# Half of a depthwise convolution by scaled copies and adding transfers, in a two-layer decoder trunk

## The chip, the cores and the metric

The kernel runs on one core of a Trainium2 chip. The metric is the time of one execution on the device in microseconds (us). The kernel before took 1113.77 us in the median of 3 runs (1112.04 to 1114.65).

The core has five engines with queues of their own, which work side by side and wait for each other by semaphores: TensorE (PE in the profile) multiplies matrices, VectorE (DVE) and ScalarE (ACT) work elementwise, GpSimd (POOL) does so more slowly, and SyncE (SP) issues transfers. ScalarE and GpSimd can issue transfers too. Each queue is worked off in its order: an instruction that waits holds up all behind it on its engine.

## The reference

The program is a decoder trunk of two layers over 528 tokens (512 and 16 learned ones in front) with 1024 channels. The first layer's mixer runs forgetting attention (8 heads of 64) beside a convolution branch; the second's pools over windows. Behind each stands a gated MLP. The part that matters here is the convolution branch, with 512 channels and 31 taps:

```
a, g = jnp.split(glu, 2, axis=-1)
u = a * jax.nn.sigmoid(g)
u = causal_depthwise_conv(u, conv_w, conv_b)     # 31 taps, each channel by itself
u = jax.nn.silu(layer_norm(u, ln_g, ln_b))       # mean and variance over the 512 channels
return jnp.concatenate([attn, u], axis=-1) @ w_out.astype(h.dtype)
```

All of it is in float32, and the sum over the taps of a channel is

```
out[c, t] = b[c] + sum over j of w[j, c] * u[c, t - 30 + j],   j = 0 .. 30
```

## The kernel before

Channels lie on the 128 partitions, tokens along the free dimension. The 512 channels of the convolution are four groups of 128, numbered 0 to 3; `u[i]` is a group's gated input with 30 zeros in front, `cv[i]` its sum. `cv[0]` to `cv[3]` are the tiles of the residual `h[0]` to `h[3]`, which are free meanwhile; in the rows below they are called `h_64` to `h_67`, so `h_65` is group 1 and `h_67` group 3, and `u_235` and `u_237` are their inputs.

All products of float32 matrices are made of three products of high and low parts. Each block of eight 128x128 weight tiles comes by one transfer of 512 KB (`raw`), is cut to its high part `wH` on ScalarE or VectorE, and its low part `wL` is the difference, on VectorE or, for the blocks listed in `POOL_CHUNKS`, on GpSimd (line 178). Most blocks of the first layer are in that list. Blocks are prepared two ahead of their use.

TensorE's order in the first layer is written out by hand. First come eight tiles of the gated input (`a` and `g` of the groups in turn, 16 half tiles), then by `PE_ORDER` 24 half tiles of queries, keys and values (F), between them the steps of the attention, and the steps of the layer norm of the convolution: SUM, MEAN, VAR, SILU. MEAN is a matmul with ones over the sum of the four `cv` tiles; it stands behind the last F. The output projection (O) follows. The instructions of the other engines are ordered by a scheduler.

When a group's gated input is ready (`done_g`, line 478), its 31 taps are entered in one of two lists. List 0 is VectorE's: one instruction for a tap, `cv = u * w + cv` (line 494). List 1 is for ScalarE with GpSimd: a product on ScalarE into a buffer `tapp`, of which there are two (line 497), and an addition to `cv` on GpSimd (line 498). The first tap of a group is on ScalarE in either case, with the bias (line 492). Groups 0 and 2 are in list 0, group 1 in list 1, and of group 3 the first 3 taps (`TAPS3`) are in list 1 and the other 28 in list 0. That makes 88 taps on VectorE and 32 additions on GpSimd.

The taps are drawn from the lists by `fill`, behind each half tile of a projection: `PACE` says how many from each list, with one pair of numbers for the gated stage and one for each later part of `PE_ORDER`. SUM draws what is left, and the sums over the groups follow on GpSimd (lines 757 and 767).

Of the kernel before, what the change touches and what calls it, by code (L numbers as in the profile page):

```python
# [52 lines left out]
# output projection in two passes: (tile of the output, tiles of the contraction)  # L53
OUT_ORDER = [(m, (0, 1, 2)) for m in range(8)] + [(m, (4, 5, 6, 7, 3)) for m in range(8)]
# first tile of the output projection whose halves take PSUM from both pools
OUT_WIDE = 3
OUT_JOINT = 1
# tiles of the convolution branch split by VectorE alone
SPLIT_V = (0, 3)
POOL_CHUNKS = (6, 7, 8, 10, 13, 14, 15, 16, 17, 18, 19, 20, 21, 22, 23, 24, 25, 28, 31, 34, 97, 98, 100, 101, 102, 104, 105, 106, 107)  # L60
# what the tensor engine does after the gated tiles. F: half a tile of an input projection, O: of the
# output projection; steps of the attention by pair of heads; a stroke: the next entry of PACE.
# [4 lines left out]
# first tiles of an up projection that go through the contraction side by side; tiles that leave PSUM  # L67
# before the norm is known
OUTER = (0, 4)
RAW = (7, 7)  # L70
# last tiles of the output, done by halves of the tokens; their stores: first and last tile, whether GpSimd
# computes them, whether ScalarE's queue takes them
HALVED = (6, 7)
OUT_PARTS = (((0, 4, 1, 0), (4, 8, 0, 1)), ((0, 1, 0, 0), (1, 3, 0, 1), (6, 8, 1, 0), (3, 6, 0, 1)))
# loads at the start: the input tile behind which the gate's weights are split, behind which the first
# weights come, the weights in front of which the table comes, tiles split by VectorE alone
START = (0, 0, 2, (1, 5))
# tiles of the pooling whose residual sum goes to GpSimd
POOL_RES = (1, 2, 3, 4, 5, 7)
POOL_Z = (1, 4, 6)  # L80
# tiles that the norm scales by halves as it comes
# [3 lines left out]
# steps of the pooling by tile: scale by the norm, window, its first tokens, residual, the next product  # L85
POOL_ORDER = ("Z0 Z1 S0 T1 D0 S1 Z2 T0 Z3 X0 S3 S2 D1 T2 T3 D2 X1 D3 Q0 Z4 Z5 S4 S5 X2 T4 T5 D4 Z6 X3 D5 Z7 "
              "S6 X4 Q2 Q5 Q1 S7 T7 T6 X5 D6 D7 X6 Q4 Q3 Q6 X7 Q7")
# taps of the convolution begun behind half a tile of a projection, on VectorE and on ScalarE with GpSimd
PACE = ((0.75, 0.25), (3.75, 5.0), (2.5, 4.5), (5.25, 1.25), (4.0, 1.0), (3.25, 3.0))
# squares of the last tiles that go to the norm by themselves: before the mixer, the MLPs and the pooling  # L90
# [4 lines left out]
# engines of the copies for a pair of heads: q twice, k twice, v (A: ScalarE, V: VectorE, P: GpSimd)  # L95
COPIES = ('AAAAA', 'VAAAV', 'APAAA', 'PAPAV')
# weight chunks whose high part VectorE takes
VECTOR_CHUNKS = (2, 3, 6, 9, 10, 14, 26, 27, 29, 30, 31, 33, 34, 96, 100, 101, 102, 105, 106, 107)
# products of constants that raise the tensor engine's clock while the first loads run
WARM = 12  # L100
# taps of the last tile of channels that go to GpSimd
TAPS3 = 3


def weight_order():
    """Order in which the tensor engine takes the 128x128 weight tiles."""
# [21 lines left out]
def trunk_kernel(  # L128
# [70 lines left out]
    def product(ps, wants, act, t0, n, first=True, final=True):  # L199
        """ps[:, half, :n] = sum over the wanted weight tiles of weight.T @ act."""  # L200
# [25 lines left out]
    def after(late, early):  # L226
        """Issue late behind early on their engine."""
        tc.add_manual_dep(late.ins, early.ins.name,
                          mybir.DependencyInfo(mybir.DependencyClass.NoSync, mybir.DependencyReason.DATA),
                          reason="order")  # L230

    def use_log_exp(early):
        """The table set with both Ln and Exp, loaded behind the instruction early."""
        ld = nc.scalar.preload_act_table_set("natural_log_exp_and_others")
        after(ld, early)
        return ld

# [1 line left out]
    def squares(m, apart, t0=0, t1=T, part=True):  # L239
        """Adds the squares of h[m] to the running sum, split at its end; the last ones stay apart."""  # L240
# [15 lines left out]
    def scaled(m, gcol, t0=0):  # L256
        """xH + xL = h[m] * g, split exactly."""
# [10 lines left out]
    def rsqrt(out, srcs, scale, bias, follow=None):  # L268
        """out = (scale * src + bias) ** -0.5: exp(-ln/2) and a Newton step. srcs: pieces in PSUM;
        follow(out, columns) comes behind each."""  # L270
# [24 lines left out]
    def inv_rms(pss, t0, early=(), follow=None):  # L295
        """R[:, token] = 1/sqrt(mean square + eps) in every partition."""
# [5 lines left out]
    # ================= layer 0: attention and convolution =================  # L302
    with ExitStack() as mx:
# [12 lines left out]
        # the gate's weights: high parts in columns 0:8, low parts from column 32 on  # L316
        # (in the memory of the attention's values, which come later)
# [24 lines left out]
        # causal masks, side by side as the blocks of the scores lie in PSUM (128 columns, 16 zeros, 128):  # L342
        # upper triangles for the maxima, lower ones for keys on partitions
# [5 lines left out]
        # the residual is read again after the mixer: until then its tiles serve as scratch  # L349
# [7 lines left out]
        # tokens on partitions: values of two heads with ones (high parts) or zeros (low) between  # L357
        # the last 16 tokens: high, high and low parts of the values below each other against high, low
        # and high parts of the weights
# [5 lines left out]
        # stacked operands of the scores. Even heads: rows 0:64 | 64:128  # L365
        #   q1 = high | low   k1 = high | high   q2 = high | decay rows   k2 = low | decay rows
        # odd heads have the two row halves exchanged.
# [53 lines left out]
        def mtile(name, wants, acts, done, alloc=(pp, pp), split_last=False):  # L421
            """Two units, one for each half of the tokens; done(half, psum) follows each."""
            ws = []
            def joint():
                """Both halves, the last weights behind the others of both."""
# [41 lines left out]
        def done_g(i):  # L467
            t_ = wk.tile([P, T], F32, tag="sq", name=f"sg{i}")

            def fn(hf, ps):  # L470
# [5 lines left out]
                if hf == 1:  # L476
                    uu = u[i][:, CW - 1:]
                    nc.gpsimd.tensor_tensor(uu, uu, t_, op=ALU.mult)
                    for j in range(CW):
                        queue[i % 2 if i < 3 or j < TAPS3 else 0].append((i, j))  # L480
# [8 lines left out]
        def tap(i, j, kind):  # L489
# [5 lines left out]
            else:  # L495
                pr = wk.tile([P, T], F32, tag="tapp", name=f"tap{i}_{j}")
                nc.scalar.activation(pr, src, AF.Copy, scale=cw(i, j))
                nc.gpsimd.tensor_tensor(cv[i], cv[i], pr, op=ALU.add)

        def fill(pace):  # L500
            for kind in range(2):
                credit[kind] = min(credit[kind] + pace[kind], len(queue[kind]))
                while credit[kind] >= 1:
                    tap(*queue[kind].pop(0), kind)
                    credit[kind] -= 1

# [1 line left out]
        def first_products():  # L508
            """The gates' logits and the first tile, as their operands come in."""
            cell["f"] = wk.tile([P, T], F32, tag="tapp", name="f")[H8, :]  # L510
            low = wk.tile([P, T], F32, tag="tapp", name="flow")[H8, :]
# [18 lines left out]
        def gate_sums():  # L530
# [6 lines left out]
            # log1p(e) = ln(1+e) + (e - ((1+e) - 1)) / (1+e)  # L537
# [62 lines left out]
        def attention(p):  # L600
            """The steps of a pair of heads by name."""
# [22 lines left out]
            # Maxima, queries on partitions. The query's own decay is the same for all its keys: it  # L624
            # stands in a row's scores and in their maximum alike, and their difference is free of it.
            def maxima(hh):
                tl = st[hh]
                N = tl["N"]
                for x, parts in enumerate((((2, 0, 272), (1, 0, 144), (0, 0, 16)), ((3, 0, 400),),
# [10 lines left out]
                    # short products in front of those whose weights load fast  # L640
# [3 lines left out]
                    # the masks cover the last columns of every block  # L644
# [32 lines left out]
            # Scores, keys on partitions; blocks of 128 keys against their causal queries.  # L677
# [517 lines left out]
```

## Time and profile before

| | |
|---|---|
| median of 3 runs | 1113.77 us (1112.04 to 1114.65) |
| span of the profiled execution, first to last instruction | 1111.1 us |
| TensorE busy | 1044.2 us, 94% |
| VectorE busy | 767.9 us, 69% |
| ScalarE busy | 467.4 us, 42% |
| GpSimd busy | 250.3 us, 23% |
| VectorE's taps, line 494 | 88, 1157 ns in the mean |
| GpSimd's additions of taps, line 498 | 32, 1566 ns in the mean |

The profiled execution is another one than the timed runs; its own time is known as its span, and the median of the runs lies 2.7 us above it. Busy shares are means over the span; the first layer's mixer, which has the convolution, takes the first 264 us or so.

How to read it: a row names the line of the program, the engine, the operation and the tiles, output in front of the arrow and inputs behind it. "x88" is a count. What stands in brackets or behind a second bar is the idle time of the engine before, and who ended it.

### The profile page before, as it was taken

How to read it: one execution, taken by the hardware profiler on the slowest of the kernel's cores; microseconds unless marked ns; L12 is line 12 of the kernel's file. 1: busy time of each engine (PE TensorE's matmuls, PEld its weight loads, DVE VectorE, ACT ScalarE, POOL GpSimd, SP SyncE). 2: the span in 40 equal slices, each digit the busy share in tenths (PEclk: the TensorE clock that was granted, in tenths of full speed). 3: DMA queues.
4: the chain of work that ended last, by engine and by line, in shares of the span. 5: the costliest groups of instructions: out<-in, count | busy, mean ns of one | idle time of the engine just before them, and what ended most of it. 6: DMA issues, size and time to landing. Idle time of an engine off the chain costs nothing. (4 is left out here: it accounts for less than half of the span.)

```text
span 1111.1 us, 19833 instructions
## 1 busy us (share of the span) xinstructions
PE 1044.2 (94%) x8356; PEld 1031.0 (93%) x8356; DVE 767.9 (69%) x1001; ACT 467.4 (42%) x710; POOL 250.3 (23%) x264
## 2 busy tenths in 40 slices
PE   8978699799999999999999999679999999999996
PEld 7877589799999999999999999579999999999995
DVE  7899999997727985236767546957985336767523
ACT  6435465465325553124434435333553124344422
POOL 7656766342500000000000013662000000000012
PEclk8988889999999999999999999899999999999998
DMA  6211111132332222332322222122322222222202
GB/s 222 68 56 57 39 39 40 58 98 75 104 108 96 87 87 94 96 95 79 95 95 89 84 96 77 38 77 77 112 88 91 91 96 95 96 96 81 92 20 76
DMA packets 28665, 93.21 MB, mean 84 GB/s; under 512 B 3616, under 2 KB 5664, under 8 KB 28576
## 3 DMA queue, kind: packets, MB, share of 16 engines
q1 hardware_dynamic: 26720, 90.68, 24.9%
q8 instruction: 66, 1.08, 0.4%
q10 hardware_dynamic: 1344, 1.23, 0.3%
q0 software_dynamic: 512, 0.03, 0.1%
q14 instruction: 23, 0.19, 0.0%
HBM read 89.80 MB, written 2.10 MB: 83 GB/s over the span
## 5 line engine op out<-in xcount | busy, mean ns | idle before, releaser
L197 PE MATMUL up<-xL,wH 128*128 128x264 f32 (+1 forms) x1408 | 287.9, 286 | 14.7 <-DVE xL L259 14.7
L197 PE MATMUL up<-xH,wH 128*128 128x264 f32 (+1 forms) x1408 | 286.5, 285 | 1.1 <-ACT xH L258 1.1
L197 PE MATMUL up<-xH,wL 128*128 128x264 f32 (+1 forms) x1408 | 287.4, 286 | 0.0
L223 ACT CAST wH<-raw 128x1024 fp32r<-128x1024 f32 x142 | 149.0, 1049 | 235.9 <-PE dn L197 120.4
L178 DVE TENSOR_TENSOR wL<-raw,wH 128x1024 fp32r<-128x1024 f32 x133 | 164.0, 1233 | 105.9 <-ACT wH L223 101.8
L197 PEld LDWEIGHTS up<-xL,wH 128*128 128x128 f32 x1408 | 220.4, 191 | 16.0 <-DVE xL L259 16.0
L197 PEld LDWEIGHTS up<-xH,wH 128*128 128x128 f32 x1408 | 220.7, 191 | 1.4 <-ACT xH L258 1.4
L197 PEld LDWEIGHTS up<-xH,wL 128*128 128x128 f32 x1408 | 220.4, 191 | 0.0
L197 PE MATMUL dn<-gH,wL 128*128 128x264 f32 (+1 forms) x704 | 145.4, 283 | 0.0
L197 PE MATMUL dn<-gH,wH 128*128 128x264 f32 (+1 forms) x704 | 145.3, 284 | 0.0
L197 PE MATMUL dn<-gL,wH 128*128 128x264 f32 (+1 forms) x704 | 145.2, 283 | 0.0
L248 POOL TENSOR_TENSOR acc<-acc,sq 128x528 f32<-128x528 f32 (+1 forms) x30 | 45.1, 1504 | 413.1 <-ACT sq L246 412.7
L922 DVE SCALAR_TENSOR_TENSOR t<-u,par,t 128x528 f32<-128x528 f32 (+1 forms) x176 | 132.7, 769 | 2.4 <-ACT t L919 0.4
L197 PEld LDWEIGHTS dn<-gL,wH 128*128 128x128 f32 x704 | 110.2, 189 | 0.1
L197 PEld LDWEIGHTS dn<-gH,wH 128*128 128x128 f32 x704 | 109.9, 188 | 0.1
L197 PEld LDWEIGHTS dn<-gH,wL 128*128 128x128 f32 x704 | 109.7, 188 | 0.0
L952 DVE TENSOR_TENSOR u<-up,R 128x528 f32<-128x528 f32 (+1 forms) x74 | 51.7, 701 | 77.6 <-PE up L197 75.3
L494 DVE SCALAR_TENSOR_TENSOR h<-u,par,h 128x528 f32<-128x528 f32 x88 | 101.1, 1157 | 0.8
L178 POOL TENSOR_TENSOR wL<-raw,wH 128x1024 fp32r<-128x1024 f32 x29 | 75.3, 2598 | 71.3 <-ACT wH L223 30.0
L919 ACT ACTIVATE t<-u,par 128x528 f32<-128x528 f32 (+1 forms) x88 | 71.4, 821 | 10.1 <-DVE gL L215 6.3
L973 DVE TENSOR_TENSOR h<-dn,h 128x528 f32<-128x528 f32 (+1 forms) x30 | 21.0, 700 | 65.4 <-PE dn L197 65.4
L944 POOL MEMSET u<- 128x2 f32 x44 | 4.0, 101 | 263.1 <-DVE t L922 260.8
(248 smaller groups left out, 1646.2 us busy)
## 6 DMA issues: line engine op xcount, KB each, us to landing
raw<-wts SPq DMA_DIRECT2D x162, 512.0 KB, 3.4
h<-hT SPq DMA_DIRECT2D x8, 264.0 KB, 5.6
hm<-hT SPq DMA_DIRECT2D x8, 264.0 KB, 4.7
outT<-y ACTq DMA_DIRECT2D x1, 512.0 KB, 3.1
outT<-y SPq DMA_DIRECT2D x1, 512.0 KB, 3.9
par<-par SPq DMA_DIRECT2D x1, 476.5 KB, 6.5
outT<-y ACTq DMA_DIRECT2D x1, 384.0 KB, 2.8
outT<-y SPq DMA_DIRECT2D x1, 256.0 KB, 2.2
```

The costliest lines, as they stand in the source:

```text
L178: eng.tensor_tensor(wL, raw, wH.bitcast(F32), op=ALU.subtract)
L197: nc.tensor.matmul(out, lhsT, rhs, start=start, stop=stop)
L223: return nc.scalar.copy(out, src)
L248: state["sum"] = nc.gpsimd.tensor_tensor(acc[:, t0:t1], acc[:, t0:t1], sq[:, t0:t1], op=ALU.add)
L494: nc.vector.scalar_tensor_tensor(cv[i], src, cw(i, j), cv[i], op0=ALU.mult, op1=ALU.add)
L919: nc.scalar.activation(t_, uu[:, off + 2:off + 2 + nt], AF.Identity, scale=col(c0 + 2), bias=col(c0 + 3))
L922: nc.vector.scalar_tensor_tensor(t_, uu[:, off + x:off + x + nt], col(c0 + x), t_, op0=ALU.mult, op1=ALU.add)
L944: nc.gpsimd.memset(uu[:, 0:2], 0.0)
L952: nc.vector.tensor_tensor(v2(ud), ps[:, :, :nu], v2(R[:, tu:tu + 2 * nu]), op=ALU.mult)
L973: nc.vector.tensor_tensor(v2(h[m][:, td:]), ps[:, :, :nd], v2(h[m][:, td:]), op=ALU.add)
```

## The change

- All 31 taps of groups 1 and 3 are entered in list 1, those of groups 0 and 2 in list 0. VectorE has 60 taps, and ScalarE makes 60 products.
- A product is added to `cv` by a transfer that GpSimd issues (`accum_op=ALU.add`): it fetches the product and the sum from SBUF and writes the new sum. GpSimd adds no tap itself.
- From list 1, `fill` takes the first entry that belongs to another group than the one taken last, as long as there is one. So groups 1 and 3 alternate as soon as both are in the list.
- The buffers `tapp` are four instead of two, here and where else the tag is used.
- `PACE` has other numbers, and GpSimd's memory for descriptors is set to 8192 bytes of a partition.

Comments are left out in the changed file, so its lines are numbered up to 2 lower or higher than before: the taps on VectorE are line 492, the products 495, the transfers 496.

```diff
-PACE = ((0.75, 0.25), (3.75, 5.0), (2.5, 4.5), (5.25, 1.25), (4.0, 1.0), (3.25, 3.0))
+PACE = ((0.75, 0.5), (2.25, 2.6), (2.25, 2.6), (2.25, 2.6), (2.25, 2.6), (3.25, 3.0))
...
                     for j in range(CW):
-                        queue[i % 2 if i < 3 or j < TAPS3 else 0].append((i, j))
+                        queue[i % 2].append((i, j))
...
             else:
-                pr = wk.tile([P, T], F32, tag="tapp", name=f"tap{i}_{j}")
+                pr = wk.tile([P, T], F32, tag="tapp", name=f"tap{i}_{j}", bufs=4)
                 nc.scalar.activation(pr, src, AF.Copy, scale=cw(i, j))
-                nc.gpsimd.tensor_tensor(cv[i], cv[i], pr, op=ALU.add)
+                nc.gpsimd.dma_start(cv[i], pr, accum_op=ALU.add)
...
                 while credit[kind] >= 1:
-                    tap(*queue[kind].pop(0), kind)
+                    last = state.get("tapped")
+                    at = next((x for x, t in enumerate(queue[kind]) if kind and t[0] != last), 0)
+                    state["tapped"] = queue[kind][at][0] if kind else last
+                    tap(*queue[kind].pop(at), kind)
                     credit[kind] -= 1
...
-    nc = bacc.Bacc("TRN2", target_bir_lowering=False, num_devices=1)
+    nc = bacc.Bacc("TRN2", target_bir_lowering=False, num_devices=1, dynamic_dma_scratch_size=8192)
```

What this does to the queues shows at three places. The first is GpSimd's queue around the multiplication that makes group 3's gated input (`u_237`), before the change; `tap_8` is the product of tap 8 of group 1.

```order
L178 TENSOR_TENSOR wL_866<-raw_863,wH_865 128x1024
L498 TENSOR_TENSOR h_65<-h_65,tap_7_952 128x528
L478 TENSOR_TENSOR u_237<-u_237,sg_351 128x528
L498 TENSOR_TENSOR h_65<-h_65,tap_8_955 128x528
L498 TENSOR_TENSOR h_65<-h_65,tap_9_958 128x528
L498 TENSOR_TENSOR h_65<-h_65,tap_10_961 128x528
```

The same place on GpSimd after the change; DMA is the issue of a transfer.

```order
L476 TENSOR_TENSOR u_237<-u_237,sg_351 128x528
L496 DMA h_67<-tap_1_908 128x528
L496 DMA h_65<-tap_5_947 128x528
L496 DMA h_67<-tap_2_950 128x528
L496 DMA h_65<-tap_6_987 128x528
L496 DMA h_67<-tap_3_990 128x528
L496 DMA h_65<-tap_7_993 128x528
L496 DMA h_67<-tap_4_1034 128x528
L496 DMA h_65<-tap_8_1037 128x528
L176 TENSOR_TENSOR wL_1153<-raw_1150,wH_1152 128x1024
```

Where a run of additions to one group stood, transfers to group 3 (`h_67`) and group 1 (`h_65`) alternate, and the subtraction for the next block of weights (`wL`) stands behind eight of them. Four transfers to group 1, taps 1 to 4, are in front of this place.

The second place is GpSimd's queue before the mean of the layer norm (`mu`), before the change. It stands there behind the casts of the keys (`k`).

```order
L224 CAST k_1_0_221<-h_69 64x528
L224 CAST k_1_1_227<-h_69 64x528
L757 TENSOR_TENSOR mu_2407<-h_66,h_67 128x528
L719 CAST P_202<-P_202 16x16
L767 TENSOR_TENSOR mu_2405<-mu_2405,mu_2407 128x528
```

The same place on GpSimd after the change:

```order
L496 DMA h_65<-tap_29_2270 128x528
L496 DMA h_67<-tap_26_2318 128x528
L496 DMA h_65<-tap_30_2321 128x528
L496 DMA h_67<-tap_27_2324 128x528
L759 TENSOR_TENSOR mu_2461<-h_64,h_65 128x528
L496 DMA h_67<-tap_28_2424 128x528
L496 DMA h_67<-tap_29_2427 128x528
L496 DMA h_67<-tap_30_2430 128x528
L759 TENSOR_TENSOR mu_2463<-h_66,h_67 128x528
L769 TENSOR_TENSOR mu_2461<-mu_2461,mu_2463 128x528
```

Before, the last additions of taps on GpSimd were far in front of the sums. Now the transfers run up to them, and the last three belong to one group.

The third place is ScalarE's queue at the first pair of heads, before the change: `P` and `PH` are exponentials of the scores, `rec` the reciprocal of their sums, `wH` the high part of a block of weights.

```order
L223 CAST wH_1527<-raw_1525 128x1024
L497 ACTIVATE tap_23_1111<-u_235,par 128x528
L223 CAST k_1_0_221<-h_69 64x528 x2
L223 CAST k_1_1_227<-h_69 64x528 x2
L734 ACTIVATE rec_0_256_1472<-o_0_256_1458 64x272
L497 ACTIVATE tap_24_1114<-u_235,par 128x528
L714 ACTIVATE PH_1_0_1478<-s_1_0_1476 128x384
L716 ACTIVATE P_1_0_1477<-s_1_0_1476 128x384
L714 ACTIVATE PH_1_1_1490<-s_1_1_1488 128x272
L716 ACTIVATE P_1_1_1489<-s_1_1_1488 128x272
```

The same place on ScalarE after the change:

```order
L718 ACTIVATE P_0_3_1345<-s_0_3_1344 128x416
L495 ACTIVATE tap_9_1255<-u_237,par 128x528
L495 ACTIVATE tap_13_1258<-u_235,par 128x528
L221 CAST wH_1500<-raw_1498 128x1024
L221 CAST k_1_0_221<-h_69 64x528 x2
L221 CAST k_1_1_227<-h_69 64x528 x2
L736 ACTIVATE rec_0_256_1445<-o_0_256_1431 64x272
L495 ACTIVATE tap_10_1261<-u_237,par 128x528
L716 ACTIVATE PH_1_0_1451<-s_1_0_1449 128x384
```

The high part of the weights stands behind two products instead of in front of one. Products (`tap`) of groups 1 and 3 now stand between the attention's steps up to the sum; before, they were those of group 1 and two of group 3, and ended well in front of it.

## Rows read from the trace of the kernel before

**Rows 1.** The page's head: span, and the busy time of two engines.

```profile
span 1111.1 us, 19833 instructions
PE 1044.2 (94%) x8356; PEld 1031.0 (93%) x8356; DVE 767.9 (69%) x1001; ACT 467.4 (42%) x710; POOL 250.3 (23%) x264
```

**Rows 2.** Stretches: us; busy us of PE, PEld, DVE, ACT, POOL; clock, DMA share, GB/s.

```profile
40.00:85.00 45.00, 36.33 (x267) 35.49 (x266) 44.61 (x44) 14.18 (x21) 29.32 (x23) 0.92 0.20 60
85.00:232.00 147.00, 122.22 (x909) 116.14 (x908) 143.70 (x221) 76.83 (x162) 85.59 (x66) 0.91 0.18 58
232.00:264.00 32.00, 31.59 (x256) 29.80 (x256) 29.26 (x65) 24.06 (x52) 10.90 (x9) 1.00 0.11 34
300.00:320.00 20.00, 20.00 (x166) 20.00 (x165) 5.87 (x6) 3.76 (x6) 5.19 (x2) 1.00 0.37 118
```

**Rows 3.** TensorE's waits, 40 to 232 us: us in total, times, longest; first, last.

```profile
PE ps_g L197 <- DVE u L464: 8.7, 4, 3.7
...
PE o L197 <- DVE VL L617: 0.9, 1, 0.9
```

**Rows 4.** One line's instructions, VectorE's taps: ns shortest, median, longest; starts.

```profile
L494 DVE SCALAR_TENSOR_TENSOR h<-u,par,h x88: 732/768/3942, 42.4 to 222.4; 128x528 f32<-128x528 f32 x88
```

**Rows 5.** Groups by line, VectorE's taps, 50 to 80 and 200 to 230 us.

```profile
L494 DVE SCALAR_TENSOR_TENSOR h<-u,par,h 128x528 f32<-128x528 f32 x21 | 28.7, 1375 | 0.4
...
L494 DVE SCALAR_TENSOR_TENSOR h<-u,par,h 128x528 f32<-128x528 f32 x13 | 10.4, 800 | 0.1
```

**Rows 6.** Stretches, VectorE's taps (line 494) alone: VectorE busy.

```profile
40.00:85.00 45.00, 35.08 (x27) 0.92 0.20 60
85.00:232.00 147.00, 66.02 (x62) 0.91 0.18 58
```

**Rows 7.** Timeline, VectorE and GpSimd near 204.7 us: start, duration, engine.

```profile
204.70 2.38 DVE L662 CAST E<-N 128x5 fp32r<-128x5 f32 x1
...
204.66 2.39 POOL L178 TENSOR_TENSOR wL<-raw,wH 128x1024 fp32r<-128x1024 f32 x1 [2.95 <-ACT wH L223]
```

**Rows 8.** Groups by line, GpSimd's additions of taps.

```profile
L498 POOL TENSOR_TENSOR h<-h,tap 128x528 f32<-128x528 f32 x32 | 50.1, 1566 | 18.3 <-ACT tap L497 9.9 <-PE ps_g L197 7.1
```

**Rows 9.** Stretches, GpSimd's additions of taps (line 498) alone: GpSimd busy.

```profile
40.00:85.00 45.00, 11.07 (x7) 0.92 0.20 60
85.00:232.00 147.00, 39.04 (x26) 0.91 0.18 58
```

**Rows 10.** One line's instructions, ScalarE's products of taps.

```profile
L497 ACT ACTIVATE tap<-u,par x32: 718/736/743, 60.6 to 165.3; 128x528 f32<-128x528 f32 x32
```

**Rows 11.** Timeline of GpSimd: gated input, one-row transfer, last sum for the mean.

```profile
85.60 1.58 POOL L478 TENSOR_TENSOR u<-u,sg 128x528 f32<-128x528 f32 x1
...
129.20 0.55 POOL L589 DMA_DIRECT2D k<-fH  x1
...
225.45 1.73 POOL L767 TENSOR_TENSOR mu<-mu,mu 128x528 f32<-128x528 f32 x1
```

**Rows 12.** DMA issues: queue, count, KB each, median us from issue to landing.

```profile
raw<-wts SPq DMA_DIRECT2D x162, 512.0 KB, 3.4
h<-hT SPq DMA_DIRECT2D x8, 264.0 KB, 5.6
hm<-hT SPq DMA_DIRECT2D x8, 264.0 KB, 4.7
...
outT<-y SPq DMA_DIRECT2D x1, 256.0 KB, 2.2
...
k<-fH POOLq DMA_DIRECT2D x8, 2.1 KB, 1.6
...
outT<-y SPq DMA_DIRECT2D x1, 128.0 KB, 1.7
```

**Rows 13.** Timeline of TensorE: the mean's matmuls.

```profile
231.83 1.05 PE L197 MATMUL mu<-mu,ones 128*128 128x264 f32 x4
```

More of the change, by code (lines that the diff above doesn't have):

```diff
@@ L100 @@
 WARM = 12
-TAPS3 = 3
 def weight_order():
@@ L503, in fill @@
                 while credit[kind] >= 1:
-                    tap(*queue[kind].pop(0), kind)
+                    last = state.get("tapped")
+                    at = next((x for x, t in enumerate(queue[kind]) if kind and t[0] != last), 0)
+                    state["tapped"] = queue[kind][at][0] if kind else last
+                    tap(*queue[kind].pop(at), kind)
                     credit[kind] -= 1
         def first_products():
-            cell["f"] = wk.tile([P, T], F32, tag="tapp", name="f")[H8, :]
-            low = wk.tile([P, T], F32, tag="tapp", name="flow")[H8, :]
+            cell["f"] = wk.tile([P, T], F32, tag="tapp", name="f", bufs=4)[H8, :]
+            low = wk.tile([P, T], F32, tag="tapp", name="flow", bufs=4)[H8, :]
             pss = [sp(f"zf{hf}")[0:40, :TH] for hf in range(2)]
@@ L778, in ln_mean @@
             for i in range(NCONV):
-                s_ = wk.tile([P, T], F32, tag="tapp", name=f"csq{i}")
+                s_ = wk.tile([P, T], F32, tag="tapp", name=f"csq{i}", bufs=4)
                 nc.scalar.activation(s_, cv[i], AF.Square)
```

## The prediction

> **What bounds the kernel now.** I read the page's head first: TensorE is busy for 94% of a 1111.1 us span, VectorE for 69% [rows 1]. Over the whole span that says TensorE. The change touches only the layer with the convolution, though, so the next view is the busy time of the engines by stage [rows 2]. Look at the two stretches from 40 to 232 us: VectorE is busy for 44.61 of 45 us and for 143.70 of 147 us, 98% in both, while TensorE rests and its granted clock is 0.91 to 0.92. Between 300 and 320 us, where nothing starves it, TensorE runs at clock 1.00 and starts 166 matmuls in 20 us, 8.3 per us. At that rate the 267 + 909 = 1176 matmuls of the two stretches would need 142 us; they take 192. So 50 us are lost there, partly as waits and partly as slow clock. The view of who TensorE waited for [rows 3] has nine lines, from 8.7 us down to 0.9 us, and every one names VectorE. In this stage VectorE sets the pace.
>
> The third step is to ask why VectorE is full. A tap (line 494) has a median of 768 ns but a maximum of 3942 ns [rows 4]; between 50 and 80 us the 21 taps average 1375 ns, between 200 and 230 us the 13 taps there average 800 ns [rows 5]. In the first stretch GpSimd adds taps, in the second it adds none. The timeline shows the mechanism at its plainest [rows 7]: a cast of 128x5 numbers on VectorE lasts 2.38 us, because GpSimd's subtraction of two SBUF operands began 0.04 us before it and held on for 2.39 us; both end within 0.03 us of each other. GpSimd work with two SBUF inputs thus takes time from VectorE. The Trainium skill states this as a rule (SBUF — State Buffer, "SBUF: two separate sides": the pair of ports shared by the two engines is an exclusive lock held for a whole instruction); the trace agrees, and the numbers below come from the rows.
>
> **What it takes away.** *VectorE's taps.* There are 88 now, 62 x 2 = 124 less the 4 first taps on ScalarE less the 32 of GpSimd. Afterwards there are 60, for channel groups 0 and 2. 28 taps at their undisturbed 768 ns are 21.5 us. *GpSimd's adds.* 32 additions at 1566 ns, 50.1 us in all [rows 8], each with two SBUF operands, 11.07 us of them before 85 us and 39.04 us behind [rows 9]. The 88 taps cost 35.08 + 66.02 = 101.1 us [rows 6] where 88 x 768 ns would be 67.6 us: 33.5 us of lock time lie on the taps alone, and VectorE's other work carries more. The adds are 50.1 of GpSimd's 29.32 + 85.59 us of work in the two stretches, 44%, and a larger part of its work with two operands, so I put what their going gives back at 20 to 35 us. VectorE falls from 188 us of 192 to some 132 to 147 us, level with TensorE's 142. It stops being the bound by itself.
>
> **What it adds.** *ScalarE*: 60 products instead of 32, 28 x 736 ns [rows 10] = 20.6 us on top of 14.18 + 76.83 us. With 112 us of work it still has room. *GpSimd's queue*: 60 transfers are issued in place of 32 adds. The rows of before have only one-row transfers on this queue; they hold GpSimd for 0.55 us, in the midst of busy VectorE [rows 11]. A transfer of 128 rows has more to prepare; I take 0.8 us, between 0.55 us and the 1.57 us that an add cost. Sixty of them are 48 us against 50.1 us: no change in GpSimd's own time. *Transfers on the engines*: 60 x 264 KB, read twice and written once; the transfer engines are 18 to 20% busy here [rows 2], so there is space.
>
> *The new wait.* This is the term that decides. Each transfer reads and writes the tile it adds to, so it can start only when the previous one for the same channel group has landed. The order on GpSimd alternates groups 1 and 3 and puts four taps of group 1 ahead; then 30 links of group 3 follow one another, 26 of them with a tap of group 1 between, up to the sum for the layer norm's mean. Their price is the time from issue to landing, which no row shows for an adding transfer. From below: 1.6 us for 2.1 KB on this queue [rows 12]. From above: 4.7 us for 264 KB when eight are queued at once. Between them, SyncE's stores take 1.7 us for 128 KB and 2.2 us for 256 KB, so 0.5 us for each 128 KB: a plain transfer of 264 KB would be 1.6 + 1.0 = 2.6 us, one that fetches both operands 1.6 + 2.1 = 3.7 us. I take 3.4 us, nearer the upper of the two because the adding must fetch both and because weight loads of 512 KB (3.4 us each) share the engines. The Trainium skill (DMA: Bandwidth & Descriptors, "Anatomy of one DMA — SWDGE (gpsimd) path") gives a fit of 2.0 us plus the bytes at 436 GB/s for a plain transfer, 2.6 us here; by it the chain would be no bound, which is the first rival. No run here shows it for one that adds.
>
> Behind a transfer that waits, GpSimd's whole queue stands: low parts of weights, which TensorE needs, small casts and fills, and in turn the products on ScalarE, since a product may overwrite its buffer only when the transfer four before it has landed. In front of the exponentials ScalarE therefore waits as well. GpSimd's other work between 85 and 232 us is 85.59 - 39.04 = 46.6 us. Between two links the queue has 3.4 - 2 x 0.8 = 1.8 us free, 47 us over 26 pairs, just as much; an order fixed in advance uses perhaps half of it, so I add 23 us.
>
> **The sum**, from the profiled execution's 1111.1 us.
> - 40 to 85 us: GpSimd adds 11.07 us here; VectorE gets about half of it back: 6 us less.
> - 85 us (group 3's gated channels are ready: the multiplication at 85.60 us [rows 11]) to 232 us (the mean's matmul at 231.83 us [rows 13]): the chain takes 30 x 3.4 = 102 us, the rest of GpSimd 23 us, the last sums 3 us as now (1.73 us for the last one [rows 11]): 128 us instead of 147, 19 us less. TensorE alone would need 909 / 8.3 = 110 us, so the chain ends last.
> - From the mean on nothing changes: TensorE is busy for 31.59 of 32 us [rows 2], and the rest of the program moves up as a whole.
> Together 25 us: 1086 us of span. The median of the three runs, 1113.77 us, lies 2.7 us over the profile's span; with that the forecast is 1089 us.
>
> Edits at no cost: SyncE's queue keeps its order. Four buffers for the products instead of two, and half the memory for descriptors, take no time as such; if that memory filled, an issue would wait for a landing, which the slow rival prices. The squares of the layer norm get the four buffers too, behind a TensorE that isn't waiting.
>
> **The rivals.**
> 1. *The landing is hidden; TensorE is the bound.* At 2.6 us the chain is 78 us, with 23 and 3 us 104 us, below TensorE's 110. Then both stretches run at 8.3 matmuls per us: 50 us less, 1064 us. For it: every TensorE wait names VectorE. Against it: the attention's steps depend on each other over three engines, and a full rate through them is unlikely.
> 2. *The landing is slow; GpSimd's queue takes VectorE's place, and the kernel is slower.* The break-even over both stretches is a middle of 153 us: (153 - 26) / 30 = 4.2 us per link. At the 4.7 us of the queued 264 KB loads the chain is 141 us; with more free time in the queue I add 15 and 3 us: 159 us, 12 us more, less 6 us before: 1120 us. At 5.6 us, the longest median for such a size [rows 12], 168 + 15 + 3 = 186 us: 1147 us. For it: nobody has shown an adding transfer here, and weights stand in the same queue. Against it: 2.2 us for a store of 256 KB.
> 3. *VectorE holds up the issues.* Each of the 56 issues behind the multiplication would wait for a VectorE operation in flight, 0.77 us, 43 us on GpSimd: 171 us for the middle, 18 us more in all, 1132 us. The row speaks against it: issues of 0.55 us beside a VectorE that never rests. In the Trainium skill (SBUF — State Buffer, the box on VectorE blocking transfers) GpSimd cannot write descriptors while VectorE runs a two-port operation; the one-row transfers here don't show it.
> 4. *Gain and loss cancel*: the chain at its break-even of 4.2 us, 1112 to 1116 us.
>
> **Chances.** The forecast 0.53, by itself 1072 to 1108 us (2.8 to 4.0 us per link); TensorE as the bound 0.14; slow landing 0.20; held-up issues 0.07; cancelled 0.06. About 0.2% (2 us) is what a measurement can tell from no change. Faster 0.53 + 0.14 = 0.67, same 0.06, slower 0.27. From 1066 to 1126 us some 0.07 is left out below and 0.13 above.
>
> **What would show it.** VectorE's taps near 0.8 us from 50 us on, 60 of them, and VectorE clearly under 90% busy up to the mean. TensorE's waits naming ScalarE or GpSimd instead. Transfers into the group's tile at 3 to 4 us to landing, 0.6 to 1.1 us of GpSimd each. The mean's matmul near 207 us. Were it later than 232 us, the term of the landing was too small; were VectorE still full, the lock was no matter of the adds; waits of the exponentials or of weights on a transfer would show the queue behind the chain to cost more than 23 us.

## The result, and the profile after

The changed kernel takes 1130.26 us in the median (1128.73 to 1132.43), the kernel before 1113.28 us (1112.04 to 1114.65) in the same comparison: a ratio of 1.0156 [1.0144, 1.0169] (in brackets the interval of 95%), 17 us slower. Forecast were 1089 us, in a range of 1066 to 1126. The slow rival, a long landing with GpSimd's queue in VectorE's place, is the one that came.

The page's head, which answers to [rows 1]:

```profile
span 1128.8 us, 19901 instructions
PE 1033.9 (92%) x8356; PEld 1021.4 (90%) x8356; DVE 713.6 (63%) x973; ACT 484.8 (43%) x738; POOL 246.0 (22%) x292
```

VectorE has 54 us less to do. Where that went is seen in the stretches, beside [rows 2]:

```profile
40.00:85.00 45.00, 38.65 (x303) 37.98 (x301) 43.78 (x48) 13.25 (x20) 23.49 (x21) 0.96 0.35 86
85.00:232.00 147.00, 109.46 (x877) 104.22 (x877) 91.75 (x192) 97.50 (x194) 83.64 (x91) 0.89 0.73 144
206.00:250.00 44.00, 0.00 (x0) 0.00 (x0) 0.42 (x1) 9.42 (x13) 17.60 (x18) 0.54 0.71 151
250.00:285.00 35.00, 33.95 (x262) 31.91 (x262) 28.62 (x62) 22.62 (x50) 10.19 (x9) 0.95 0.05 16
```

From 85 to 232 us VectorE's work fell from 143.70 to 91.75 us. In the third line TensorE starts no matmul in 44 us, and no engine is near full: that is not an engine's limit but something everybody waits for. The transfer engines, 18% busy from 85 to 232 us before, are 73% busy. TensorE's longest waits from 40 to 290 us, beside [rows 3], name it:

```profile
PE mu L195 <- POOL mu L769: 44.8, 1, 44.8
PE ps_g L195 <- DVE u L462: 5.9, 2, 5.6
```

The timeline shows the mean's matmuls, with the wait in brackets, where before they began at 231.83 us without one [rows 13]:

```profile
250.39 2.13 PE L195 MATMUL mu<-mu,ones 128*128 128x264 f32 x4 [44.84 <-POOL mu L769]
```

TensorE came to this place at 250.39 - 44.84 = 205.6 us, 26 us earlier than before, and left it 18.6 us later. From there on nothing differs: 1128.8 - 250.4 = 878.4 us to the end, before 1111.1 - 231.8 = 879.3 us. So the whole loss is made in front of this matmul. One line's instructions show who made it: VectorE's taps [rows 4] and the transfers on GpSimd.

```profile
L492 DVE SCALAR_TENSOR_TENSOR h<-u,par,h x60: 731/762/7774, 43.3 to 142.7; 128x528 f32<-128x528 f32 x60
...
L496 POOL DMA_DIRECT2D h<-tap x60: 607/862/1219, 63.6 to 244.3; - x60
...
  DMA h<-tap: 51.6, 19
...
DMA to landing us min/median/max: 3.3/3.9/6.9
```

VectorE's half is summed at 143 us. The transfers go on to 244 us, and GpSimd idled 51.6 us, in 19 waits for a landing. The transfers of one group form a chain: each waits until the one before has landed, and a link is the time from one issue to the next. At the end of the chain GpSimd's timeline holds little else:

```profile
229.34 0.86 POOL L496 DMA_DIRECT2D h<-tap  x1 [0.68 <-DMA h<-tap]
231.21 1.29 POOL L759 TENSOR_TENSOR mu<-h,h 128x528 f32<-128x528 f32 x1 [1.01 <-DMA h<-tap]
233.18 0.87 POOL L496 DMA_DIRECT2D h<-tap  x1 [0.68 <-DMA h<-tap]
240.45 0.88 POOL L496 DMA_DIRECT2D h<-tap  x1 [6.40 <-DMA h<-tap]
244.29 0.87 POOL L496 DMA_DIRECT2D h<-tap  x1 [2.96 <-DMA h<-tap]
247.68 1.29 POOL L759 TENSOR_TENSOR mu<-h,h 128x528 f32<-128x528 f32 x1 [2.52 <-DMA h<-tap]
249.04 1.29 POOL L769 TENSOR_TENSOR mu<-mu,mu 128x528 f32<-128x528 f32 x1
```

Read the starts: from 229.34 to 233.18 and from 240.45 to 244.29 a link took 3.84 us, 3.3 to landing and 0.53 until the next issue. From 233.18 to 240.45 it took 7.27 us: in that stretch the eight loads of the residual (hm) were on the engines too. The list of DMA issues, beside [rows 12], has the medians:

```profile
raw<-wts SPq DMA_DIRECT2D x162, 512.0 KB, 3.4
h<-tap POOLq DMA_DIRECT2D x60, 264.0 KB, 3.9
...
hm<-hT SPq DMA_DIRECT2D x8, 264.0 KB, 6.4
...
k<-fH POOLq DMA_DIRECT2D x8, 2.1 KB, 3.4
```

The median of the one-row transfers (`k<-fH`) mixes two kinds: the four before 50 us land after 1.5 to 2.6 us, the four between 120 and 167 us, issued behind adding transfers that had not landed, after 4.1 to 5.8 us. Before the change, four one-row transfers beside a weight load alone landed after 1.5 to 2.0 us. In the middle of the chain there is a second kind of delay, in GpSimd's queue:

```profile
113.87 0.86 POOL L496 DMA_DIRECT2D h<-tap  x1 [4.40 <-DMA h<-tap]
115.17 0.86 POOL L496 DMA_DIRECT2D h<-tap  x1 [0.44 <-DVE h L580]
115.73 2.70 POOL L176 TENSOR_TENSOR wL<-raw,wH 128x1024 fp32r<-128x1024 f32 x1
118.05 1.22 POOL L496 DMA_DIRECT2D h<-tap  x1
...
128.09 2.40 POOL L176 TENSOR_TENSOR wL<-raw,wH 128x1024 fp32r<-128x1024 f32 x1 [0.68 <-ACT wH L221]
130.43 0.85 POOL L496 DMA_DIRECT2D h<-tap  x1
```

The first, fourth and last lines are group 3. The transfers of 118.05 and 130.43 us come right behind a subtraction for the weights: it sits ahead of them in program order, although their predecessors had landed 0.9 and 1.9 us before. These two also land late, after 6.9 and 5.4 us, and that is no coincidence. SyncE's waits from 40 to 260 us show why:

```profile
SPq L171 <- POOL wL L176: 142.2, 14, 16.7
```

A load of weights waits until a subtraction has freed its buffer. Of the 12 loads issued from 85 to 232 us ten begin within 0.03 us of the end of a subtraction on GpSimd, at 118.46 and 130.52 us for instance, and the transfers behind it in GpSimd's queue are issued within 0.6 us of it. So the queue sends each of these transfers off together with 512 KB of weights.

### The profile page after: what moved, and what is told of

The parts are those of the page before. It is cut to its first block, busy times and chain, and to the rows that moved or that the text cites. A ratio compares the mean times of both kernels' runs of the same rounds, so it can differ in the third digit from the quotient of the medians.

```text
span 1128.8 us, 19901 instructions
## 1 busy us (share of the span) xinstructions
PE 1033.9 (92%) x8356; PEld 1021.4 (90%) x8356; DVE 713.6 (63%) x973; ACT 484.8 (43%) x738; POOL 246.0 (22%) x292
## 5 line engine op out<-in xcount | busy, mean ns | idle before, releaser
L176 POOL TENSOR_TENSOR wL<-raw,wH 128x1024 fp32r<-128x1024 f32 x29 | 74.0, 2554 | 51.6 <-ACT wH L221 20.2
L496 POOL DMA_DIRECT2D h<-tap x60 | 52.5, 904 | 81.7 <-DMA h<-tap 51.6
L212 ACT CAST gH<-t 128x528 fp32r<-128x528 f32 (+1 forms) x44 | 27.6, 626 | 84.1 <-DVE t L935 84.1
```

Source lines behind the costliest of these rows:

```text
L176: eng.tensor_tensor(wL, raw, wH.bitcast(F32), op=ALU.subtract)
L212: nc.scalar.copy(oH, src)
L496: nc.gpsimd.dma_start(cv[i], pr, accum_op=ALU.add)
```

## The experiments

Where no other is named, a kernel is the changed one with the edit shown; times are medians, ratios go to the kernel before in the same comparison.

**Second sums (e1).** Groups 1 and 3 get a second tile each; odd taps go there, and VectorE adds the two at the end: four chains of 14 or 15 transfers instead of two of 30.

```
...
+                to = cx[i] if j % 2 else cv[i]
+                if j == 1:
+                    nc.scalar.activation(to, src, AF.Copy, scale=cw(i, j))
+                    return
-                nc.gpsimd.dma_start(cv[i], pr, accum_op=ALU.add)
+                nc.gpsimd.dma_start(to, pr, accum_op=ALU.add)
...
+            for i in (1, 3):
+                nc.vector.tensor_tensor(cv[i], cv[i], cx[i], op=ALU.add)
```

> Each of groups 1 and 3 gets a second sum: odd taps are added into it, and VectorE adds the two sums at the end. Four chains of 14 or 15 links instead of two of 30, the same products. If the landings in a row are what made the kernel slower (5.4 us a link, 161 us for the 30 of group 3), a chain of 15 is done long before TensorE comes to the mean, which then lies near 207 us instead of 250 us, TensorE's wait for the mean falls from 44.8 us to under 6 us, and the time is 1085 to 1095 us. If GpSimd's and ScalarE's queues were what filled the 161 us (60 issues, products and weights in turn), the mean stays later than 235 us and the time over 1115 us.

Measured: 1091.67 us, ratio 0.9805 [0.979, 0.9819], the first answer. The issues and the mean's matmuls:

```profile
h<-tap POOLq DMA_DIRECT2D x30, 264.0 KB, 5.1
cx<-tap POOLq DMA_DIRECT2D x28, 264.0 KB, 5.5
...
210.94 1.16 PE L195 MATMUL mu<-mu,ones 128*128 128x264 f32 x4
```

A single landing is longer than in the changed kernel (5.1 and 5.5 against 3.9 us), yet the bracket in front of the mean is gone. So it was the dependence from link to link that cost the time, not the transfers' load as such. Of the kernels that leave nothing out it is the fastest.

**Transfers that copy (e2).**

```
-                nc.gpsimd.dma_start(cv[i], pr, accum_op=ALU.add)
+                nc.gpsimd.dma_start(cv[i], pr)
```

> The transfers copy instead of adding (the sums over the taps of groups 1 and 3 are left out); the order on every engine and the waits are the changed kernel's. If the latency of any transfer of this size from this queue makes the link, an undisturbed landing goes from 3.3 us to 2.6 to 3.0 us and the time to 1105 to 1120 us. If the adding itself makes it, the landing falls to 2.0 us or less and the time to about 1090 us.

Measured: 1117.28 us in one run. A landing came to 2.2 us at least and 2.6 in the median, an issue to 0.54 us; TensorE still waited:

```profile
PE mu L195 <- POOL mu L769: 38.3, 1, 38.3
```

The time is the first answer's, the landing lies between the two. The adding makes the shortest landing 1.1 us longer (3.3 against 2.2); without it this run is still 4 us slower than the kernel before. How that can be is taken up below.

**The other division (e3).** The kernel before, with its order and division, but its 32 adds as transfers (with the changed kernel's four buffers and memory for descriptors).

```
-                nc.gpsimd.tensor_tensor(cv[i], cv[i], pr, op=ALU.add)
+                nc.gpsimd.dma_start(cv[i], pr, accum_op=ALU.add)
```

> The division of taps and the pace of the kernel before (group 1 and three taps of group 3 by products, 88 taps on VectorE); only the 32 additions on GpSimd become adding transfers, with four buffers. If GpSimd's additions held VectorE up by the shared ports, VectorE's taps average 0.85 us instead of 1.16 us, and as one chain of 30 links begun at 64 us ends by 205 to 215 us, the kernel gets faster than before: 1090 to 1100 us. If VectorE is relieved only by the number of its taps, nothing is gained: 1110 us or more.

Measured: 1121.03 us, ratio 1.0066 [1.0049, 1.0084]: a miss by 20 us and more. VectorE's taps fell to 947 ns in the mean, but TensorE waited at the mean. The wait, VectorE's last taps and the last sum over two groups:

```profile
PE mu L197 <- POOL mu L767: 32.7, 1, 32.7
...
213.35 23.40 DVE L494 SCALAR_TENSOR_TENSOR h<-u,par,h 128x528 f32<-128x528 f32 x28 [5.57 <-DMA h<-tap]
...
236.83 1.29 POOL L757 TENSOR_TENSOR mu<-h,h 128x528 f32<-128x528 f32 x1 [15.93 <-DVE h L494]
```

Group 1's chain of 30 ran from 62.6 to 219.1 us, 5.2 us a link, 4 us behind the end that was expected. What the expectation left out came later. The two transfers of group 3 stand near the end of the list; the second was issued at 210.0 us, and only when it had landed did VectorE's 28 taps of group 3, which add to the same tile, begin. They ended at 236.8 us, and the sums and the mean followed. With half the transfers a link costs about as much; but the time of this kernel is that of VectorE's taps behind two late transfers, and does not show what the chain alone would have cost.

**No adds (e4).** The kernel before without GpSimd's 32 adds.

```
-                nc.gpsimd.tensor_tensor(cv[i], cv[i], pr, op=ALU.add)
```

> The kernel before with GpSimd's 32 additions of taps left out (their products are still made, but not added). It measures by itself what the additions cost: if they hold VectorE up, its 88 taps average 0.85 us instead of 1.16 us and the time falls by 15 to 30 us, to 1083 to 1098 us. If VectorE was full of its own taps, the time stays within 5 us of before.

Measured: 1094.87 us, ratio 0.9835 [0.9819, 0.9852], the mean at 212.1 us, VectorE's 88 taps down from 101.1 [rows 6] to 80.5 us, 935 ns each in the mean, where 0.85 us was named. So 18 us were to be had from GpSimd's adds alone, before any tap leaves VectorE: what the change takes away was worth taking. (The run also frees VectorE's taps of group 3 from the adds of that group, which stand in front of them; the two parts aren't told apart.)

**Seven buffers (e5).**

```
-                pr = wk.tile([P, T], F32, tag="tapp", name=f"tap{i}_{j}", bufs=4)
+                pr = wk.tile([P, T], F32, tag="tapp", name=f"tap{i}_{j}", bufs=7)
...
```

> The changed kernel with seven buffers for ScalarE's products instead of four (one use of each buffer is a product that waits for its adding transfer). Theory: the sum of group 3 is one chain of transfers into one tile, each issued only when the one before has landed, so more finished products only wait longer in front of it: 30 links of 5.4 us as before, TensorE's wait at the layer norm's mean stays at 40 to 46 us, and the time stays at 1130 (1125 to 1134). Rival: ScalarE's waits for a free buffer (40.0 us in the changed kernel, longest 5.3) hold the chain up; with seven buffers a link would come down toward its 3.3 to 3.9 us landing, the chain would end 40 us earlier and the time would be 1090 to 1100.

Measured: 1130.66 us, ratio 1.0151 [1.0132, 1.0169], the wait at the mean 44.2 us, as expected. ScalarE waits for a buffer 31.2 us instead of 40.0, and the chain ends 1.3 us earlier: this wait is a consequence and costs next to nothing here.

**Adds at the new division (e6).**

```
-                nc.gpsimd.dma_start(cv[i], pr, accum_op=ALU.add)
+                nc.gpsimd.tensor_tensor(cv[i], cv[i], pr, op=ALU.add)
```

> The changed kernel's division of the taps and its order, but every product is added by GpSimd (58 to 60 adds) and not by a transfer. Theory: the adds take GpSimd 60 x 1.57 = 94 us, beside VectorE's taps, which they hold up again (mean tap well above the 0.77 us of the changed kernel, toward 1.1 to 1.4); GpSimd's 147 us between 85 and 232 then hold the adds and some 45 us of other work, so the last add comes near 230, the mean near 232, and the time is 1108 to 1122: near the kernel before, and less than the changed kernel, although VectorE is slower in it. Rival, that the division (30 of group 3's taps on the slow side, none on VectorE) is at fault and not the transfers' landing: no better than the changed kernel, 1127 to 1145.

Measured: 1131.01 us, ratio 1.0151 [1.0131, 1.017], the second answer. The groups of both engines and TensorE's wait:

```profile
L492 DVE SCALAR_TENSOR_TENSOR h<-u,par,h 128x528 f32<-128x528 f32 x60 | 77.0, 1295 | 0.7
L496 POOL TENSOR_TENSOR h<-h,tap 128x528 f32<-128x528 f32 x60 | 91.1, 1540 | 19.7 <-ACT tap L495 18.7
...
PE mu L195 <- POOL mu L769: 21.2, 1, 21.2
```

VectorE's taps are held up again (1295 ns, against 1019 in the changed kernel), and GpSimd's 60 adds end as late as the transfers. TensorE itself comes to the mean 22 us later than in the changed kernel, at 227.7 us, as VectorE is slower; the mean's matmul begins at 248.8 us. At this division adding transfers and adds cost the same, by different routes; 28 more taps on the side that must sum one after another, with the order and the pace that go with them, are a part of the loss, whichever way they are added.

**Half the bytes (e7).**

```
-                nc.gpsimd.dma_start(cv[i], pr, accum_op=ALU.add)
+                nc.gpsimd.dma_start(cv[i][:, :TH], pr[:, :TH], accum_op=ALU.add)
```

> The changed kernel, but every adding transfer carries only the first 264 of the 528 columns (132 KB in place of 264); the other half of those sums is left out. It asks what a link's 5.4 us are made of. Theory: a part that bytes set, since landings rise from 3.3 us alone to 5.7 to 6.9 beside a 512 KB weight load and fall from 3.3 to 2.3 when nothing is added; halved, a landing would be 2.4 to 2.8 us alone and 3.5 to 4.5 beside a load, a link 3.5 to 4.2, group 3's chain 30 x 3.8 = 114 us from 86 to about 200, the mean comes near 206 to 212 and the time is 1088 to 1100. Rival: the price is per transfer, whatever it carries (a queue's turn behind the weight loads and the way to the semaphore): landings stay at a median of 3.7 to 3.9, the wait at the mean stays over 30 us, and the time is 1118 to 1130.

Measured: 1120.0 us, ratio 1.0056 [1.004, 1.0072], TensorE's wait 31.1 us. Neither answer is right: time and wait are the rival's, but the landing did fall, to a median of 3.0 us, and the time by 10 us. The table takes the chains of this run and four others apart, link by link. It sums group 3's 30 transfers: landings are issue to landing, gaps are landing to the next issue of the group.

| kernel | first issue to last landing | landings (mean) | gaps | mean's matmul |
|---|---|---|---|---|
| changed | 86.5 to 247.6 | 133.3 (4.44) | 27.8 | 250.4 |
| e7, half the bytes | 84.6 to 235.2 | 114.1 (3.80) | 36.6 | 238.0 |
| e2, copies | 82.3 to 233.2 | 105.0 (3.50) | 45.9 | 236.0 |
| e9, freed queue | 85.6 to 231.4 | 122.7 (4.09) | 23.1 | 234.3 |
| e10, both | 81.3 to 203.7 | 91.0 (3.03) | 31.4 | 206.6 |

In the changed kernel the 13 landings that no load touches, of weights or of the residual, average 3.4 us; the 14 that lie beside loads for over 2 us average 5.6 us, and for ten of these the load is one that a subtraction in front of the transfer let go. That the two groups' transfers meet each other costs little: of both chains, the 24 landings with another transfer of taps beside them and no load average 3.5 us, while the two beside loads alone for over 2 us (issued at 74.01 and 233.18 us) took 6.1 and 6.7 us. And when landings shrink, gaps grow: in e2, 31 of the 46 us lie beyond the usual gap of 0.53 us, and 26 us of the gaps are filled by other instructions of GpSimd's queue, 20 of them by subtractions for the weights.

**A freed queue (e9).** VectorE does the subtractions of chunks 13 to 34.

```
-POOL_CHUNKS = (6, 7, 8, 10, 13, 14, 15, 16, 17, 18, 19, 20, 21, 22, 23, 24, 25, 28, 31, 34, 97, ...
+POOL_CHUNKS = (6, 7, 8, 10, 97, ...
```

> The changed kernel, but the low parts of weight chunks 13 to 34 that GpSimd subtracts (wL from raw and wH, 12 of them of 2.3 to 2.9 us between 80 and 250 us) go to VectorE, so that they no longer stand in GpSimd's queue between the transfers. In the changed kernel group 3's chain of 30 links is 133 us of landings and 28 us between a landing and the next issue, 13 of these beyond the least gap. Theory of two terms (landings lengthened by the weight loads; GpSimd's queue in front of the issue): the landings stay near 133 to 140, the excess of the gaps falls from 13 to 2 to 5, the chain ends near 236 to 240 and the time is 1117 to 1125. Rival, the landings alone: what the queue delays only moves a transfer into or out of a weight load, so a shorter gap is given back by longer landings, and the time stays at 1127 to 1133. Second rival: VectorE, with 15 us more of work, is late for the weights that TensorE wants, 1133 or more.

Measured: 1116.39 us, ratio 1.0032 [1.0021, 1.0043], 14 us less than the changed kernel and 0.6 us under the range named. The direction is that of two terms, the split isn't: gaps fell by 5 us, landings by 11, with 11 instead of 14 beside loads for over 2 us. Queue and loads aren't independent: a subtraction in GpSimd's queue also decides when the next load begins. The mean's matmul shows a limit that comes next:

```profile
234.25 2.13 PE L195 MATMUL mu<-mu,ones 128*128 128x264 f32 x4 [8.60 <-POOL mu L769]
```

TensorE waits here for 8.6 us only, because it comes to the mean at 225.7 us instead of 205.6: 11 of these 20 us are longer waits for ScalarE's work of the attention (17 us in all, up to 7.5 us at a time, instead of 6). At 206.40 us, for instance, a product that had waited 3.5 us for a landing stands right in front of the exponentials. So the attention is now almost as late as the chain.

**Both (e10).** The edits of e2 and e9 together.

> Both terms made small at once: the transfers copy and do not add (the sums of those taps are left out), and GpSimd's twelve subtractions of weight chunks go to VectorE. With the copying transfers alone the landings of group 3's chain came to 105 us (near the 102 of the prediction), but the gaps rose to 46, 31 of them beyond the least one, 28 behind GpSimd's queue. Theory of two terms: landings 103 to 108, gaps 15 + 3 to 8, the chain ends near 82 + 125 = 207, the mean is ready at 210 to 214, and the time is 1090 to 1098. Rival (something third, as ScalarE's products in their program order, paces the links): the chain still ends after 220, and the time is 1105 to 1117.

Measured: 1091.82 us, ratio 0.9812 [0.9797, 0.9826]. The matmuls of the mean in the copying kernel and in this one:

```profile
235.97 2.13 PE L195 MATMUL mu<-mu,ones 128*128 128x264 f32 x4 [38.26 <-POOL mu L769]
```

```profile
206.59 2.13 PE L195 MATMUL mu<-mu,ones 128*128 128x264 f32 x4 [9.78 <-POOL mu L769]
```

With the chain at 91 + 31 = 122 us, close to the 102 + 23 = 125 us of the prediction, mean and time come out as forecast (206.6 for 206.8 us; 1092 for 1089 us). The two terms differ, only their sum agrees. So the frame of the forecast held (a chain that ends this early does give this time), and its two prices did not. Either edit alone gives 13 to 14 us, the two together 38.

**Both on top of the second sums (e11).** The edit of e9 in e1.

> The kernel with a second sum for groups 1 and 3 (1091.7 us, where TensorE no longer waits for the mean) with GpSimd's twelve subtractions given to VectorE as well. If TensorE and its waits for VectorE (ps_g 6.4, o 5.0 us) set that kernel's time, a quicker queue of GpSimd brings nothing and VectorE's 15 us more may cost: 1089 to 1097. If the four chains' transfers still hold the end of the sums, it is 2 to 5 us faster: 1086 to 1090.

Measured: 1094.07 us, ratio 0.9838 [0.9823, 0.9852]; 2 us above e1, the first answer. A quicker queue of GpSimd brings nothing there.

**Fewer links (e8, e12).** The last ten taps of group 3 (e8), or of groups 1 and 3 (e12, with `i % 2` for `i == 3`), go to VectorE behind all others.

```
-                        queue[i % 2].append((i, j))
+                        (tail3 if i == 3 and j >= 21 else queue[i % 2]).append((i, j))
...
+            for i, j in tail3:
+                tap(i, j, 0)
```

> The changed kernel with the last ten taps of group 3 given to VectorE, in one piece behind all other taps (VectorE's own taps end near 143 us in the changed kernel). It asks whether the time follows the number of links. Theory (a link of the lone chain costs 5.4 us, 30 links run from 86.5 to 247.6): 20 links end near 86.5 + 20 x 5.4 = 195, ten taps of 0.77 us come behind (203), the sums of the mean at 206, so TensorE finds the mean ready near 206 to 210: time 1088 to 1097, about 35 to 40 us under the changed kernel. Rival: something other than the chain sets the mean (the queue of GpSimd, which would still issue 50 transfers, or the loads that follow): 1110 to 1130.

Measured: 1121.96 us, ratio 1.007 [1.0053, 1.0087], the mean at 237.6 us: a miss. Group 3's 20 links did end at 200.2 us, at 5.7 us a link, but group 1's 30 links, which I had left out of the sum, ran from 61.9 to 233.6 us, as in the changed kernel (63.6 to 231.1 us). I had cut one chain of two equally long ones.

> The changed kernel with the last ten taps of group 1 as well as of group 3 given to VectorE, behind all its other taps: 40 transfers, two chains of 20 links. With group 3's chain alone cut, group 1's 30 links (61.9 to 233.6 us, 5.7 us each) ended last. Theory (the time follows the longest chain): both chains end by 63 + 20 x 5.7 = 177 to 200 us (group 3's 20 links ended at 200 in that run), 20 taps of 0.77 us come behind, 15 us, the mean is ready near 210 or before TensorE comes to it (205 to 212): 1086 to 1096 us. Rival (the transfers of a pair of chains are not what sets the mean; the program order in which GpSimd and ScalarE meet the sum's place is): the wait at the mean stays over 15 us and the time over 1105.

Measured: 1104.12 us, ratio 0.9917 [0.9901, 0.9933]: faster than before, 8 us above what I named. The two chains of 20 ended at 179.6 and 202.4 us, but TensorE waited again:

```profile
PE mu L195 <- POOL mu L772: 11.4, 1, 11.4
...
212.82 7.54 DVE L493 SCALAR_TENSOR_TENSOR h<-u,par,h 128x528 f32<-128x528 f32 x7
```

VectorE takes its twenty late taps among the attention's work and ends them at 220.4 us. The chains were the limit down to here; then VectorE's tail is.

## Why the prediction was wrong

**What was removed** was right in size. VectorE fell to 43.78 + 91.75 = 135.5 us in the two stretches, where 132 to 147 were said; the taps behind 85 us average 25.77 us / 32 = 805 ns in the stretches of line 492 alone. TensorE's waits for VectorE up to the mean fell from 33 us (the nine lines of [rows 3]) to 11 us, it reached the mean 26 us earlier, and e4 shows 18 us for GpSimd's adds by themselves.

```profile
40.00:85.00 45.00, 34.63 (x29) 0.96 0.35 86
85.00:145.00 60.00, 25.77 (x32) 0.91 0.75 154
```

**The first stretch's 6 us** did not come to the chain. Before 85 us a tap still averages 34.63 / 29 = 1194 ns. The adds were gone, but GpSimd's other work with two operands was not: the longest tap, 7.77 us from 48.02 us on, spans two subtractions and a gate's product that GpSimd ran one after another from 49.47 to 55.22 us. GpSimd began group 3's multiplication at 83.31 us instead of 85.60 [rows 11], and the first link was issued at 86.53 us, where the sum implied about 79.

**The failed step is the chain's "30 x 3.4 = 102 us" plus "the rest of GpSimd 23 us".** Against the mean at 206.8 us (231.8 less 25) the measured 250.4 us is 43.6 us late: some 7.7 from the late start, 133.3 - 102 = 31.3 from the landings, 27.8 - 23 = 4.8 from the gaps; the last sums took the 3 us that were said. The landing is the large one. 3.4 us was right for a transfer that meets no load (3.4 on average) but I took it for the mean while naming the weight loads beside it; 14 of the 30 links lie beside loads and average 5.6 us. And the two terms aren't independent, as the sum had them: a subtraction in the queue holds the next transfer and then lets a load go beside it. [rows 12] had the hint: the 264 KB loads that are queued together take 4.7 and 5.6 us.

The 23 us were nearly right by accident. The argument was that the queue's other work partly fits into the waits; with landings as short as those assumed it fits less, and the gaps are 46 us (e2). In e2, whose landings sum to 105 us and so nearly to the assumed 102, the time is still 28 us above the forecast. A chain of 30 links through an in-order queue pays landing and queue together: 161.1 / 30 = 5.4 us a link, where 4.2 was the break-even.

**The rivals.** The first (TensorE the bound) needed landings of 2.6 us; e2 had that median and still waited. The second came, and its formula was too kind as well: at 4.44 us it gives 133 + 15 + 3 = 151 us for the middle, 2 us under the break-even of 153; the late start and the longer gaps make the rest. The third, VectorE holding up issues, did not show: an issue has a median of 0.86 us over the chain and takes 0.87 to 0.88 us from 233 to 245 us, where VectorE does next to nothing. In the Trainium skill (SBUF — State Buffer, the box on VectorE blocking transfers) GpSimd cannot write a transfer's descriptors while VectorE runs a two-port operation; no issue here is longer than 1.22 us, so for this mix of operations the trace does not show it. Nor does an issue show a wait for the halved memory for descriptors. One part of the change was not varied by itself: the pace at which the products are drawn. In the changed kernel GpSimd waited for a product 8.3 us in five waits, so little hangs on it there; what another pace would give is open.

## What to carry to other kernels

A sum built from adding transfers is a chain: price a link as landing under the load that runs beside it, plus restart, plus what stands ahead in the issuing queue, and compare the whole chain with the time at which its sum is wanted; several sums, added at the end, hide it. Look at every chain that ends near the same place before cutting one. Taking work off the engine that sets the pace helps only as far as the next dependence allows; here four chains in place of two turned 17 us lost into 21 us won.

## What the hardware showed

- An adding transfer of 264 KB within SBUF landed in 3.3 us at best, a copying one in 2.2; their issues held GpSimd for 0.86 and 0.54 us. With half the columns an adding landing is 2.7 us at best, so that by these two points some 2 us of the 3.3 do not depend on the bytes (an estimate).
- The next issue came 0.28 us behind a landing at the least and 0.53 us as a rule.
- A transfer that met no load landed in 3.4 us on average, beside loads of 264 or 512 KB in 5.6 us; the weight loads from 85 to 232 us, 3.4 us in the median before, took 4.3 us.
- Over TensorE's rest (206 to 250 us) the granted clock averages 0.54, near the lower of its two levels (1.2 of 2.4 GHz), and the mean's first matmuls behind it took 647 ns; in e1, without the rest, 386 ns. The four of them took 2.13 us instead of 1.05 [rows 13]: this costs about a microsecond.
